# Five of seven Strassen products doubled in the first projection, and stick-breaking sums over later keys taken as two split products

## The chip, the cores and the metric

The program runs on one core of one Trainium2 chip. The metric is device time in microseconds (us) of that core; the changed kernel is timed against the kernel shown here. Engines are named as in the profile: PE is the matrix engine's matmul row and PEld its weight loads, DVE the vector engine, ACT the scalar (activation) engine, POOL the GpSimd engine, SP the engine that issues most DMAs; q behind a name means its instruction queue.

## What is computed

One decoder layer over 512 tokens of width 2048, in float32. Cut to what matters here:

```python
h = rmsnorm(x, attn_norm_g)
proj = h @ w_in                       # 2048 x 9216: u, v_sgu, q, k, v_att, g_a, g_b
y_a = chunked_spatial_gating(gelu(u), rmsnorm(gelu(v_sgu)))
y_b = stick_breaking_attention(rmsnorm(q), rmsnorm(k), v_att)   # 8 heads of 128
x = x + (sigmoid(g_a) * (y_a @ w_up_a) + sigmoid(g_b) * (y_b @ w_up_b)) @ w_o
x = x + swiglu(rmsnorm(x))            # w_ffn_in 2048 x 11264, w_ffn_out 5632 x 2048
x = x + sigmoid(rmsnorm(x) @ w_ple_gate) * (p @ w_ple)

# in stick_breaking_attention, for a block of 128 queries:
z = q @ k.T * scale
log_1m = where(key < query, log_sigmoid(-z), 0)
tail = cumsum(log_1m, reverse=True) - log_1m      # the sum over later keys
w = where(key < query, exp(log_sigmoid(z) + tail), 0)
y = w @ v
```

## The kernel before

All activations are held transposed, features on the partitions and the 512 tokens along the row. A float32 operand is kept as two float32r parts: `hi`, a rounded copy made by ACT, and `lo`, the rest, made by DVE as source minus `hi`. A product of two operands is then three matmuls: hi·hi, hi·lo and lo·hi (`mm3`, L271 to L273).

**Units.** The five big products are cut into units that give 256 output features each. A unit runs over 8 forms (256 input features each). A form of kind "S" is prepared for Strassen's scheme: 7 products of 128x128 weight blocks with 128x256 activation blocks instead of 8. Weights come by two SP DMAs and a POOL DMA that adds to what has landed (L316, L318, L338); `Weights.steps` makes two more sums on DVE (L350) and splits everything (`whi` on ACT, L334; `wlo` on DVE, L331). Weights of two forms are handled together, so a unit consists of 4 calls of `Pair.add`, each with 7 products for two forms.

**Two ways of a product.** Where `Pair.doubled` is false, `add` calls `mm3` on 256 columns three times for each product and form, into half a bank of PSUM; `HALVES` says which half of the banks "a", "q", "z" and "y", so that a unit holds four banks. Where it is true (only the feed-forward input, w_ffn_in), the activation's hi and lo parts lie side by side, and one matmul of 512 columns with the hi weights gives both hi·hi and hi·lo into the two halves of a bank of the product's own (L628); a second one of 256 columns with the lo weights adds to the first half.

**Combining.** During the last `add` of a unit, a generator (`mix`, or `mix_doubled`) is advanced after each product and adds the products up to the four output blocks: ACT copies (L653, L684) and DVE additions (L656, L687) that read PSUM. There are 6 banks "ps" and 2 banks "small"; a bank is written again by a later unit only after its readers are done.

**The first projection** (L1141 on) has 36 units: rounds 0 to 3 of q, k, v (two heads each) with 14 gate units between, then 4 s and 4 u units of the spatial gating and two more gates. The units of the first round's q, k and v run plain (8 products); the other 33 are Strassen units that are not doubled.

**Attention** runs beside those units. `tick()` is called eight times in a unit and starts what is due: `beside(generator)` advances a generator, which yields the number of ticks until its next step. `attention` handles a head's key blocks j = 3, 2, 1, 0 with (4 - j)·128 queries each. `stage_a` computes the scores (L1007, float32), their softplus on ACT and two terms on DVE (L1016, L1018) and masks on POOL (L1020). `stage_b` sums over later keys with float32 matmuls: a triangle for the block's own keys (L1030), and a matrix of ones times `later`, the running sum of later blocks (L1032); then it subtracts (L1034), keeps `later` up to date (POOL L1040, DVE L1042), takes the exponential and masks (L1045). `finish` multiplies with v (L1054).

**Storage and order.** `parts` and `wholes` are two arenas in SBUF; `take` chooses a place by first fit, aligned, from the end, or oldest given back. In a `tick` a form that is ready is fetched or built only if the arenas have room (`fits`). Instructions stand on each engine in an order fixed when the program is built: a scheduler sets it from priorities and dependences, `in_turn` chains the instructions on weights and in the mixes, and `tick` puts its own behind the unit's latest.

## Time and profile before

| what | value |
|---|---|
| runs | 2717.98, 2718.68, 2721.21 us, median 2718.68 |
| the profiled execution | 2719.95 us |
| its span, first to last instruction | 2718.3 us |
| mean granted clock of PE | 0.997 |
| PE busy | 2693.0 us, 99% of the span |
| DVE, ACT, POOL busy | 2075.1, 1353.5, 449.2 us |

The three runs differ by 3.2 us, and the profiled execution lies 1.3 us over their median. In the profile, busy time of PE comes from pipelined matmuls whose ends are modelled: a 256-column matmul shows 0.28 us but the next one begins 0.12 us later. What a matmul costs is therefore read from one start to the next. Columns in a timeline are start, duration, engine, line, operation and operands; in a table of lines, busy us, mean ns of one, and idle time before it with what ended it.

### The profile page before, as it was taken

The numbers are of one execution on the slowest core, as the hardware profiler recorded it, in microseconds if no ns is written. First come the engines' busy times: TensorE is split into PE (matmuls) and PEld (weight loads), VectorE is DVE, ScalarE is ACT, GpSimd is POOL, SyncE is SP. The second block draws the span as 40 slices with busy tenths as digits, with TensorE's granted clock in tenths as the row PEclk, the third lists the DMA queues.
The fourth block names the chain that finished last, engine by engine and source line by source line (L and its number), as shares of the span: only waits on it lengthen the run. The fifth ranks groups of instructions, "written<-read, shape, count | busy, mean of one in ns | idle before, by whom it ended". The sixth has DMA issues, their size and how long they took to land.

```text
span 2718.3 us, 45582 instructions
## 1 busy us (share of the span) xinstructions
PE 2693.0 (99%) x17243; PEld 2438.9 (90%) x17243; DVE 2075.1 (76%) x3377; ACT 1353.5 (50%) x2045; POOL 449.2 (17%) x527
## 2 busy tenths in 40 slices
PE   9999999999999999999999999999999999999999
PEld 7899999999999889988888888888888999989898
DVE  8566767667777667678889898989899567788876
ACT  7645556565554334365444444444445344453543
POOL 0222322232320000001111111111111111111110
PEclk9999999999999999999999999999999999999999
DMA  7567676767776447768888888887877669778784
GB/s 227 153 180 176 170 175 172 176 175 185 173 193 195 140 138 227 201 192 200 219 208 203 201 205 201 203 203 202 204 196 225 174 168 258 197 242 239 240 232 117
DMA packets 303132, 529.03 MB, mean 195 GB/s; under 512 B 25664, under 2 KB 162880, under 8 KB 302912
## 3 DMA queue, kind: packets, MB, share of 16 engines
q1 hardware_dynamic: 242160, 425.70, 49.0%
q0 software_dynamic: 60752, 100.43, 23.6%
q8 instruction: 135, 2.21, 0.3%
q14 instruction: 85, 0.70, 0.1%
HBM read 478.84 MB, written 47.19 MB: 194 GB/s over the span
## 4 chain that ended last, share of the span: by engine, by line
PE 95%; DMA 2%; DVE 1%; ACT 1%; issue 1%; POOL 0%; SPq 0%; ACTq 0%; DVEq 0%; POOLq 0%
PE ps L628 26%; PE ps L272 20%; PE ps L271 20%; PE ps L273 20%; PE small L628 4%; PE small L1054 1%; PE small L946 1%; PE small L1030 1%; PE small L1007 1%; DMA wholes<-x 0%; PE small L1032 0%; DMA ple<-out 0%; DVE wlo L331 0%; ACT whi L334 0%; PE small L1108 0%
## 5 line engine op out<-in xcount | busy, mean ns | idle before, releaser
L271 PE MATMUL ps<-parts,whi 128*128 128x256 f32 (+1 forms) x3995 | 1247.1, 314 | 13.3 <-ACT parts L266 7.4
L334 ACT ACTIVATE whi<-wholes 128x512 fp32r<-128x512 f32 (+4 forms) x950 | 856.1, 917 | 793.6 <-PE ps L272 305.3
L272 PE MATMUL ps<-parts,whi 128*128 128x256 f32 (+1 forms) x3960 | 1231.9, 311 | 1.3 <-DVE parts L267 1.3
L273 PE MATMUL ps<-parts,wlo 128*128 128x256 f32 (+1 forms) x3960 | 1230.4, 311 | 0.3 <-DVE wlo L331 0.3
L331 DVE TENSOR_TENSOR wlo<-wholes,whi 128x512 fp32r<-128x512 f32 (+4 forms) x950 | 964.9, 1050 | 156.5 <-ACT whi L334 155.0
L271 PEld LDWEIGHTS ps<-parts,whi 128*128 128x128 f32 x3995 | 764.2, 191 | 62.1 <-ACT parts L266 7.6
L272 PEld LDWEIGHTS ps<-parts,whi 128*128 128x128 f32 x3960 | 758.0, 191 | 44.7 <-DVE parts L267 2.2
L273 PEld LDWEIGHTS ps<-parts,wlo 128*128 128x128 f32 x3960 | 757.6, 191 | 38.9 <-DVE wlo L331 0.8
L628 PE MATMUL ps<-parts,whi 128*128 128x512 f32 x2064 | 683.2, 396 | 0.0
L628 PEld LDWEIGHTS ps<-parts,wlo 128*128 128x128 f32 x2064 | 387.9, 188 | 89.6
L628 PE MATMUL ps<-parts,wlo 128*128 128x256 f32 x2064 | 406.4, 278 | 0.0
L350 DVE TENSOR_TENSOR wholes<-wholes 128x256 f32<-128x256 f32 (+1 forms) x794 | 329.6, 415 | 27.5 <-issue 4.3
L628 PEld LDWEIGHTS ps<-parts,whi 128*128 128x128 f32 x2064 | 330.0, 189 | 2.1
L338 POOL DMA_DIRECT2D wholes<-w_ffn_in x172 | 149.7, 870 | 688.9 <-DVE wholes L350 229.7
L338 POOL DMA_DIRECT2D wholes<-w_in x132 | 118.8, 903 | 510.4 <-DMA wholes<-w_in 222.5
L687 DVE TENSOR_TENSOR out<-out,ps 128x256 f32<-128x256 f32 x258 | 107.6, 417 | 83.1 <-ACT out L684 83.0
L656 DVE TENSOR_TENSOR out<-out 128x256 f32<-128x256 f32 x59 | 25.0, 425 | 173.1 <-ACT out L653 172.8
L628 PE MATMUL small<-parts,whi 128*128 128x512 f32 x344 | 136.6, 397 | 0.0
L267 DVE TENSOR_TENSOR parts<-wholes,parts 128x1024 fp32r<-128x1024 f32 (+4 forms) x131 | 123.7, 953 | 14.0 <-ACT parts L266 13.5
L266 ACT ACTIVATE parts<-wholes 128x1024 fp32r<-128x1024 f32 (+4 forms) x131 | 105.7, 834 | 39.6 <-DVE wholes L497 15.6
L338 POOL DMA_DIRECT2D wholes<-w_ffn_out x56 | 57.0, 1031 | 401.0 <-DMA wholes<-w_ffn_out 187.5
L1299 ACT ACTIVATE out<-out 128x512 f32<-128x512 f32 x44 | 27.8, 633 | 161.2 <-DVE out L1298 161.2
(119 smaller groups left out, 1645.1 us busy)
## 6 DMA issues: line engine op xcount, KB each, us to landing
wholes<-w_ffn_in SPq DMA_DIRECT2D x172, 384.0 KB, 5.4
wholes<-w_in SPq DMA_DIRECT2D x132, 384.0 KB, 4.7
wholes<-w_ffn_in SPq DMA_DIRECT2D x172, 256.0 KB, 4.7
wholes<-w_ffn_in POOLq DMA_DIRECT2D x172, 256.0 KB, 5.2
wholes<-w_in SPq DMA_DIRECT2D x132, 256.0 KB, 3.8
wholes<-w_in POOLq DMA_DIRECT2D x132, 256.0 KB, 4.8
wholes<-x SPq DMA_DIRECT2D x32, 512.0 KB, 5.6
wholes<-w_ffn_out SPq DMA_DIRECT2D x31, 512.0 KB, 4.5
```

The source lines that it names most:

```text
L266: return (nc.scalar.activation(hi, src, AF.Copy), nc.vector.tensor_tensor(out=lo, in0=src, in1=hi.bitcast(F32), op=ALU.subtract))
L267: nc.vector.tensor_tensor(out=lo, in0=src, in1=hi.bitcast(F32), op=ALU.subtract))
L271: nc.tensor.matmul(ps[:, s], sh, mh[:, s], start=start, stop=False)
L272: nc.tensor.matmul(ps, sh, ml, start=False, stop=False)
L273: return nc.tensor.matmul(ps, sl, mh, start=False, stop=stop)
L331: in_turn(nc.vector.tensor_tensor(out=self.lo[:, blocks], in0=r, in1=h.bitcast(F32), op=ALU.subtract))
L334: in_turn(nc.scalar.activation(h, r, AF.Copy))
L338: nc.gpsimd.dma_start(out=raw[:, 3:5], in_=self.src[:, 1:3], accum_op=ALU.add)
L350: in_turn(nc.vector.tensor_tensor(out=o, in0=x, in1=y, op=ALU.add))
L628: m = nc.tensor.matmul(out, l, r, start=first and k == 0, stop=last and k == 1)
L687: in_turn(nc.vector.tensor_tensor(out=out, in0=x, in1=y, op=op))
L1299: nc.scalar.activation(g, g, AF.Silu)
```

## The change

In the first projection, the 33 Strassen units get `doubled=5`: the first five of the seven products (`PRODUCTS`) use one 512-column and one 256-column matmul each, as the feed-forward input does for all seven; the last two still use three 256-column matmuls and share the bank "y". A unit so holds six banks. `mix_doubled` combines five doubled products and that bank. `mix`, which the mixed units of later stages use, adds with three 256-column additions in place of one of 512 columns over two blocks, and needs no buffer of its own.

In attention, a block's masked terms are split into two float32r parts, `zh` (ACT, L1058) and `zl` (DVE, L1062). The sums over later keys are two float32r matmuls with a triangle of ones (L1068, L1069). The row of key 0, which no triangle of strictly later keys needs, carries later blocks' sums: POOL keeps the block's own first row (L1054) and clears it (L1055), and DVE puts into the next block's row 0 what row 0 of this block's result gives (L1071); the triangle for these blocks has ones in row 0 (`tris[1]`). `later` and the product with ones are gone. The steps go in threes of ticks through all eight blocks of a round's two heads, and attention begins 6 ticks after the k unit instead of 5 after the v unit. q is made in an `out` tile, and its normalised form goes to `y_b`.

The arenas change: `parts` is 1024 columns larger, `wholes` 512 smaller, alignment is to two places, and gates are loaded to the lowest place.

On PE, at the sums of a round's block j = 0 (`small` is the bank of the sums, `ps` a unit's bank); before:

```order
L272 MATMUL ps_1074<-parts,whi_80 128x256
L273 MATMUL ps_1074<-parts,wlo_81 128x256
L1030 MATMUL small_1305<-wholes,tri 128x512
L1032 MATMUL small_1305<-wholes,ones 128x384
L271 MATMUL ps_1103<-parts,whi_80 128x256
L272 MATMUL ps_1103<-parts,whi_80 128x256
L273 MATMUL ps_1103<-parts,wlo_81 128x256
```

and after, in such a place:

```order
L273 MATMUL ps_2941<-parts,wlo_77 128x256
L1068 MATMUL small_3121<-parts,tri_123 128x512
L629 MATMUL ps_3132<-parts,whi_80 128x512
L629 MATMUL ps_3132<-parts,wlo_81 128x256 x2
L629 MATMUL ps_3132<-parts,whi_80 128x512
L629 MATMUL ps_3137<-parts,whi_80 128x512
L629 MATMUL ps_3137<-parts,wlo_81 128x256 x2
L629 MATMUL ps_3137<-parts,whi_80 128x512
L1069 MATMUL small_3121<-parts,tri_123 128x512
L629 MATMUL ps_3142<-parts,whi_80 128x512
```

Six matmuls of a product for two forms became four, and the second product of the sums stands two products of the unit behind the first.

On DVE, the last `add` of a unit with a block of attention beside it (`out` is the unit's result, `p` its spare buffer); before:

```order
L656 TENSOR_TENSOR out_3030<-out_3030 128x256
L331 TENSOR_TENSOR wlo_81<-wholes,whi_80 128x1280
L331 TENSOR_TENSOR wlo_81<-wholes,whi_80 128x512
L656 TENSOR_TENSOR out_3030<-out_3030,p_283_3037 128x256
L656 TENSOR_TENSOR out_3030<-out_3030,p_283_3037 128x2x256
L1034 TENSOR_TENSOR wholes<-wholes,small_3067 128x512
L656 TENSOR_TENSOR out_3030<-out_3030,ps_2871 128x256
L656 TENSOR_TENSOR out_3030<-ps_2878,out_3030 128x512
```

and after, from the second addition of the mix:

```order
L688 TENSOR_TENSOR out_3066<-out_3066,ps_2909 128x256
L688 TENSOR_TENSOR out_3066<-out_3066 128x256
L688 TENSOR_TENSOR out_3066<-out_3066,ps_2914 128x256
L331 TENSOR_TENSOR wlo_79<-wholes,whi_78 128x1280
L331 TENSOR_TENSOR wlo_79<-wholes,whi_78 128x512
L688 TENSOR_TENSOR out_3066<-out_3066 128x256
L688 TENSOR_TENSOR p_347_3071<-p_347_3071,ps_2925 128x256
L1062 TENSOR_TENSOR parts<-wholes,parts 128x512
L688 TENSOR_TENSOR out_3066<-out_3066,ps_2936 128x256
L688 TENSOR_TENSOR out_3066<-out_3066,p_347_3071 128x2x256
L688 TENSOR_TENSOR out_3066<-out_3066,ps_2936 128x256
L688 TENSOR_TENSOR out_3066<-ps_2941,out_3066 128x512
```

The mix has ten DVE instructions instead of five, and the `lo` part of attention's terms (L1062) stands among them.

On SP, at the end of the first projection (`y` are attention's results, read back as operands of the next stage); before:

```order
L314 DMA wholes<-w_up_b 128x1024 x2
L1225 DMA gsp_8878<-out_8823 128x1024
L314 DMA wholes<-w_up_a 128x1024
L479 DMA wholes<-y_129 128x1024
L479 DMA wholes<-y_128 128x1024
L314 DMA wholes<-w_up_a 128x1024
```

and after:

```order
L314 DMA wholes<-w_up_b 128x1024 x2
L1253 DMA gsp_7991<-out_7939 128x1024
L314 DMA wholes<-w_up_a 128x1024
L479 DMA wholes<-y_132 128x1024
L314 DMA wholes<-w_up_a 128x1024
L314 DMA wholes<-w_up_b 128x1024
L479 DMA wholes<-y_133 128x1024
L479 DMA wholes<-y_134 128x1024
```

The last two reads of `y` stand two weight loads later.

The diff, cut:

```diff
-PARTS = 16 * PLACE
-WHOLES = 13824
+PARTS = 16 * PLACE + 1024
+WHOLES = 13312
...
-                    start = -(-start // PLACE) * PLACE
+                    start = -(-start // (2 * PLACE)) * 2 * PLACE
...
-            self.doubled = doubled and not self.n["P"]
+            self.doubled = 0 if self.n["P"] else doubled
...
-                    if self.doubled:
+                    if i < self.doubled:
                         ps = self.at(i)
                         both = ps, wh[:, w], t[:, x].rearrange("p s c -> p (s c)")
                         low = ps[:, :256], wl[:, w], t[:, x, 0]
...
-            copy(s, "q")
-            tt(b[:, 2], b[:, 1], s7)
-            tt(b[:, 1:4:2], b[:, 1:3], s5.unsqueeze(1).to_broadcast([P, 2, 256]))
+            copy(o[:, T:], "q")
+            tt(b[:, 2], b[:, 1], b[:, 2])
+            tt(b[:, 1], b[:, 1], b[:, 3])
+            tt(b[:, 3], b[:, 2], b[:, 3])
...
-            tt(c11, p2[0], c11, sub)
-            yield
-            tt(c12, p3[0], c12, sub)
-            tt(c11, c11, p2[1], add)
-            tt(c12, c12, p3[1], add)
+            if ps:
+                p2, p3 = ps
+                tt(c11, p2[0], c11, sub)
+                yield
+                tt(c12, p3[0], c12, sub)
+                tt(c11, c11, p2[1], add)
+                tt(c12, c12, p3[1], add)
+            else:
+                yield
+                tt(o[:, :T], self.at("y"), o[:, :T], sub)
...
+        def stage_m(h, j):
+            l, s, w = a_tile("l")[:, : (NT - j) * P], sums(j), weights(h, j)
             nc.vector.scalar_tensor_tensor(out=w, in0=s, scalar=0.0, in1=l,
                                            op0=ALU.min, op1=ALU.subtract)
             nc.vector.scalar_tensor_tensor(out=s, in0=s, scalar=0.0, in1=l,
                                            op0=ALU.max, op1=ALU.add)
             nc.gpsimd.affine_select(out=s[:, :P], in_=s[:, :P], pattern=[[1, P]],
...
+            if j < NT - 1:
+                if j:
+                    nc.gpsimd.tensor_copy(first(j), s[0:1])
+                nc.gpsimd.memset(s[0:1, :P], 0.0)
+
+        def stage_b(j):
+            nc.scalar.activation(zh[:, : (NT - j) * P], sums(j), AF.Copy)
+
+        def stage_c(j):
             n = (NT - j) * P
-            sp, w = state.pop((h, j))
-            later = state.get((h, "later"))
-            tp = small_bank()[:, :n]
-            nc.tensor.matmul(tp, tri, sp, start=True, stop=j == NT - 1)
-            if j < NT - 1:
-                nc.tensor.matmul(tp[:, P:], ones, later[:, j * P :], start=False,
-                                 stop=True)
+            in_turn(nc.vector.tensor_tensor(out=zl[:, :n], in0=sums(j), in1=att["zh"].f(0, n),
+                                            op=ALU.subtract))
+
+        def stage_d(h, j):
+            n, w = (NT - j) * P, weights(h, j)
+            tp, t = small_bank()[:, :n], tris[j < NT - 1]
+            nc.tensor.matmul(tp, t, zh[:, :n], start=True, stop=False)
+            nc.tensor.matmul(tp, t, zl[:, :n], start=False, stop=True)
+            if j:
+                nc.vector.tensor_tensor(out=sums(j - 1)[0:1, P:], in0=tp[0:1], in1=first(j),
+                                        op=ALU.add)
             nc.vector.tensor_tensor(out=w, in0=w, in1=tp, op=ALU.subtract)
-            if j == NT - 1:
-                later = a_tile("later", 3 * P)
-                state[h, "later"] = later
-            if j > 0:
-                c = j * P
-                nc.gpsimd.tensor_copy(later[:, c - P : c], sp[:, :P])
-                if j < NT - 1:
-                    nc.vector.tensor_tensor(out=later[:, c:], in0=later[:, c:], in1=sp[:, P:],
-                                            op=ALU.add)
             nc.scalar.activation(w, w, AF.Exp)
...
+        blocks = [(h, j) for h in range(2) for j in range(NT - 1, -1, -1)]
+        stage_a(*blocks[0])
+        yield 1
+        stage_m(*blocks[0])
+        yield 1
+        stage_a(*blocks[1])
+        for i, (h, j) in enumerate(blocks):
+            ahead = blocks[i + 1 : i + 3]
+            stage_b(j)
             yield 1
-            stage_b(h, 3)
+            if i == NT:
+                finish(0)
+            stage_c(j)
+            if ahead:
+                stage_m(*ahead[0])
             yield 1
-            stage_a(h, 1)
+            stage_d(h, j)
+            if ahead[1:]:
+                stage_a(*ahead[1])
             yield 1
...
-            yield pair(xs, last=i == len(srcs) - 1, home=lambda: block(*order[i]))
+            yield pair(xs, last=i == len(srcs) - 1, home=lambda: block(*order[i]),
+                       doubled=5)
...
+            beside(attention(i, kT, rk, a_tile("v", 1024)), 6)
...
-            s = load(gate_spill[b, j], PLACE if b == "a" and OUT[j] == "S" else 1024)
+            s = load(gate_spill[b, j], PLACE if b == "a" and OUT[j] == "S" else 1024,
+                     "low")
```

More of the change, by code (lines that the diff above doesn't have):

```diff
@@ L475, in cut, with load @@
         return x.rearrange("p (b c) -> p b c", c=256)
-    def load(src, n=1024):
-        b = take(n, "old")
+    def load(src, n=1024, how="old"):
+        b = take(n, how)
         nc.sync.dma_start(out=b.f(0, 1024), in_=src)
@@ L835, in hybrid_layer @@
     nc.vector.memset(ones, 1.0)
-    tri = consts.tile([P, P], F32, name="tri")
+    tris = [consts.tile([P, P], F32R, name=f"tri{i}") for i in range(2)]
+    tri = tmp.tile([P, P], F32, tag="diag", name="tri")
     nc.gpsimd.affine_select(out=tri, in_=ones, pattern=[[-1, P]], compare_op=ALU.is_gt,
                             fill=0.0, base=0, channel_multiplier=1)
+    nc.vector.tensor_copy(tris[0], tri)
+    nc.vector.memset(tri[0:1, :], 1.0)
+    nc.vector.tensor_copy(tris[1], tri)
     expo = consts.tile([P, 8], F32, name="expo")
@@ L931, in a_tiles @@
     def a_tiles():
-        for tag, n in (("l", T), ("later", 3 * P), ("w0", T), ("w1", 3 * P), ("w2", 2 * P), ("w3", P),
-                       ("k", 1024), ("v", 1024), ("zs", 1024)):
+        for tag, n in (("l", T), ("w0", T), ("w1", 3 * P), ("w2", 2 * P), ("w3", 2 * P),
+                       ("first", 5 * P), ("k", 1024), ("v", 1024), ("zs", 1024)):
             att[tag] = take(n)
+        for tag in ("zh", "zl"):
+            att[tag] = parts.take(T, "high")
     def a_tile(tag, n=T, start=0):
@@ L982, in q_prep @@
             yield 2
-            nc.scalar.activation(s, flip(q.f()), AF.Copy, scale=gcol[:, g_q : g_q + 1])
+            if not h:
+                y_b[i] = take(1024)
+            nc.scalar.activation(y_b[i].f(h * T, (h + 1) * T), flip(q.f()), AF.Copy,
+                                 scale=gcol[:, g_q : g_q + 1])
             give(q)
@@ L995, in v_prep, with attention, sums, weights @@
             times(v[:, h * T : (h + 1) * T], flip(o[:, h * T : (h + 1) * T]), norm1.cols)
-    def attention(rnd, qT, kT, rk, v):
+    def attention(rnd, kT, rk, v):
         state = {}
         yield 1
-        turn = [0]
+        qT = y_b[rnd].f()
+        zh, zl = (att[t].own() for t in ("zh", "zl"))
+        def sums(j):
+            return a_tile("zs", (NT - j) * P, j % 2 * T)
+        def weights(h, j):
+            return a_tile(f"w{j}", (NT - j) * P, (j == NT - 1) * h * P)
+        def first(j):
+            return (sums(j) if j == NT - 1 else a_tile("first", (NT - j) * P, (j == 1) * 2 * P))[0:1]
         def stage_a(h, j):
@@ L1203, in hybrid_layer @@
         if w == "q":
-            qT = o
-            beside(q_prep(qT))
+            beside(q_prep(o, i))
         elif w == "k":
@@ L1306, in hybrid_layer @@
     for m in range(KH):
-        o = pair(fs, last=m == KH - 1, plain=m == 0, doubled=True).out()
+        o = pair(fs, last=m == KH - 1, plain=m == 0, doubled=7).out()
         if m == 0:
```

56 lines of the change are left out of this document (16 added, 40 removed).

## The prediction

> **What bounds the kernel now.** I read the page's busy times first, then the chain that ended last, then the list of what PE waited for, and then the two stretches of the program that do Strassen units in the two ways.
>
> ```profile
> PE 2693.0 (99%) x17243; PEld 2438.9 (90%) x17243; DVE 2075.1 (76%) x3377; ACT 1353.5 (50%) x2045; POOL 449.2 (17%) x527
> ...
> PE 95%; DMA 2%; DVE 1%; ACT 1%; issue 1%; POOL 0%; SPq 0%; ACTq 0%; DVEq 0%; POOLq 0%
> ```
>
> The first row is busy time by engine, the second the shares of the chain. PE is the bound: whatever shortens its instruction stream shortens the program, as long as nothing makes it wait. What it waits for is little:
>
> ```profile
> PE small L946 <- ACT wholes L968: 2.2, 1, 2.2
> ...
> PE small L1054 <- POOL wholes L1045: 1.7, 4, 0.4
> ...
> PE small L1007 <- DVE wholes L1034: 0.2, 1, 0.2
> ```
>
> The columns are us in total, times, longest. In these three rows attention's own work holds PE for 4.1 us, of which the first round's query preparation is 2.2. No row has L1030 or L1032 waiting, the two matmuls that the change replaces.
>
> ```profile
> 125.00:835.00 710.00, 708.27 (x5636) 685.33 (x5635) 498.88 (x803) 395.72 (x725) 184.63 (x232) 1.00 0.71 178
> 1200.00:1500.00 300.00, 299.14 (x1679) 259.27 (x1678) 259.07 (x462) 152.47 (x216) 54.16 (x61) 0.99 0.85 216
> 80.00:160.00 80.00, 77.17 (x567) 72.35 (x566) 51.80 (x91) 52.41 (x120) 23.85 (x33) 0.98 0.65 166
> ```
>
> These are stretches with busy us of PE, PEld, DVE, ACT and POOL, then the granted clock. The first holds nearly all of the 33 Strassen units of the first projection: PE is busy for 708.27 of 710 us, DVE for 70%. The second lies in the feed-forward input, where all seven products are doubled: DVE is at 86%, and PE still loses less than 1 us in 300. The third contains the 2.2 us wait and has a clock of 0.98: 2% of 80 us is another 1.6 us that this stretch lost.
>
> **Doubling five products.** The price of a unit is read from unit to unit, where nothing else uses PE. In the first projection the first copy of the mix comes once in a unit:
>
> ```profile
> 801.76 0.60 ACT L653 ACTIVATE out<-ps 128x512 f32<-128x512 f32 x1 [1.00 <-PE ps L273]
> ...
> 821.92 0.60 ACT L653 ACTIVATE out<-ps 128x512 f32<-128x512 f32 x1 [0.96 <-PE ps L273]
> ```
>
> In the feed-forward input, the same place of two units in the chain:
>
> ```profile
> 1350.64 4.19 PE ps L628 x24
> ...
> 1370.16 4.19 PE ps L628 x24
> ```
>
> 20.16 us against 19.52 us: seven doubled products save 0.64 us in a unit. From one start to the next, the single matmuls say the same:
>
> ```profile
> 299.72 0.28 PE L271 MATMUL ps<-parts,whi 128*128 128x256 f32 x1
> 299.84 0.28 PE L272 MATMUL ps<-parts,whi 128*128 128x256 f32 x1
> ...
> 1389.76 0.40 PE L628 MATMUL ps<-parts,wlo 128*128 128x256 f32 x2
> 1390.00 0.63 PE L628 MATMUL ps<-parts,whi 128*128 128x512 f32 x2
> 1390.46 0.40 PE L628 MATMUL ps<-parts,wlo 128*128 128x256 f32 x2
> ```
>
> A matmul of 256 columns takes 0.12, so an old product of one form takes 0.36; two doubled ones take 1390.46 - 1389.76 = 0.70, or 0.35 each, which leaves 0.23 for 512 columns. The gain is the third weight load, not columns, of which there are 768 either way. Five of seven products give 0.64 x 5/7 = 0.46 us in a unit, and 33 units give **-15.1 us**. The ends are 0 (were it columns alone) and 15.1; I take 15.1, because the same operation with the same shapes was measured beside it.
>
> The Trainium skill speaks against this: "TensorE: Matmul & The Clock Gate", section Back-to-back issue gap, gives an isolated warm matmul N/2.4 + 2.5 ns. An estimate from that page: three of 256 columns take 327.5 ns, 512 and 256 together 325.0, so 33 x 40 products of one form would save 3.3 us. By that rule 256 columns take 109 ns; the trace has 120, and does not agree.
>
> **Attention's sums.** Before, a block's two float32 matmuls appear as four records. What they put into the stream is the distance between the first of them and the second of the unit's matmuls behind, less that unit matmul's 0.12:
>
> ```profile
> 174.55 1.02 PE L1030 MATMUL small<-wholes,tri 128*128 128x512 f32 x2
> 175.41 0.81 PE L1032 MATMUL small<-wholes,ones 128*128 128x384 f32 x2
> 175.76 0.58 PE L271 MATMUL ps<-parts,whi 128*128 128x256 f32 x1
> 176.18 0.28 PE L272 MATMUL ps<-parts,whi 128*128 128x256 f32 x1
> ...
> 161.90 0.60 PE L1030 MATMUL small<-wholes,tri 128*128 128x256 f32 x2
> 162.34 0.38 PE L1032 MATMUL small<-wholes,ones 128*128 128x128 f32 x2
> 162.48 0.36 PE L271 MATMUL ps<-parts,whi 128*128 128x256 f32 x1
> 162.68 0.28 PE L272 MATMUL ps<-parts,whi 128*128 128x256 f32 x1
> ...
> 116.49 0.39 PE L1030 MATMUL small<-wholes,tri 128*128 128x128 f32 x2
> 116.63 0.36 PE L271 MATMUL ps<-parts,whi 128*128 128x256 f32 x1
> 116.83 0.28 PE L272 MATMUL ps<-parts,whi 128*128 128x256 f32 x1
> ```
>
> That is 1.51 us for j = 0 (896 columns), 0.66 for j = 2 (384 columns) and 0.22 for j = 3 (128); j = 1 has 640 columns, and at the 1.7 ns a column of the other two takes 1.08. A head pays 3.47 us. After, the pairs of float32r matmuls have 512, 384, 256 and 128 columns: 0.46 and 0.24 for the first and third by the rows above, 0.35 for 384 between them. For 128 float32r columns there is no row; the pair lies between 0.12 (half of the 256-column one) and 0.44 (the float32 one twice), and I take 0.24, since the rows at 0.12 with one weight load each look bound by it. A head then pays 1.29, and eight heads gain 8 x 2.18 = **-17.5 us**, with ends 16 and 18.5.
>
> **What is added beside PE.** Prices from the groups by form, and medians for a line in all its sizes:
>
> ```profile
> L687 DVE TENSOR_TENSOR out<-out,ps 128x256 f32<-128x256 f32 x258 | 107.6, 417 | 83.1 <-ACT out L684 83.0
> L684 ACT ACTIVATE out<-ps 128x256 f32<-128x256 f32 x129 | 49.5, 384 | 29.4 <-PE ps L628 26.5
> L653 ACT ACTIVATE out<-ps 128x512 f32<-128x512 f32 x59 | 35.1, 595 | 41.0 <-PE ps L273 40.5
> L656 DVE TENSOR_TENSOR out<-out,p 128x512 f32<-128x512 f32 x59 | 40.8, 692 | 1.8
> L1034 DVE TENSOR_TENSOR wholes<-wholes,small x32: 280/480/689, 118.9 to 618.6; 128x128 f32<-128x128 f32 x8, 128x256 f32<-128x256 f32 x8, 128x384 f32<-128x384 f32 x8, 128x512 f32<-128x512 f32 x8
> L1012 ACT ACTIVATE wholes<-small,rr x32: 353/527/683, 110.4 to 609.0; 128x128 f32<-128x128 f32 x8, 128x256 f32<-128x256 f32 x8, 128x384 f32<-128x384 f32 x8, 128x512 f32<-128x512 f32 x8
> L1020 POOL TENSOR_SCALAR_AFFINE_SELECT wholes<-wholes 128x128 f32<-128x128 f32 x32 | 14.5, 453 | 66.0 <-DVE wholes L1018 56.5 <-PE ps L272 9.5
> L1040 POOL COPY wholes<-wholes 128x128 f32<-128x128 f32 x24 | 15.8, 660 | 1.3
> ```
>
> The mix of a unit had three DVE additions of 256 columns and two of 512 (3 x 0.417 + 2 x 0.692 = 2.64 us); it gets eight and two (4.72), so 33 units cost DVE 69 us. Attention adds 32 subtractions for `zl` (0.480 each, as L1034: 15.4) and 24 additions of one row (on average 256 columns: 10.0), and loses 16 additions to `later` (128 and 256 columns, 5.6). DVE goes from 498.88 to some 587 us in a stretch that shrinks to 677: 87%, what the feed-forward input carries with PE full. ACT gets four copies of 256 for two of 512 (+0.35 a unit) and 32 copies for `zh` (0.527 each): 424 us, 63%. POOL loses 24 copies (15.8) and gets 16 of one row and 24 clearings; with 0.66 for each that is 195 us, 29%. All of this is hidden by PE's stream; if the cover went, DVE's 69 us would be the first to show. The mixed units of later stages (36) pay 0.14 each on DVE, beside a PE that has more than enough work. A unit's six banks: the one of product i is wanted again a unit later, and its readers come within the last `add`; the feed-forward input holds its six the same way without a wait.
>
> **The new waits.** The sums now hang on a chain DVE, POOL, ACT (`zh`), DVE (`zl`), PE, and the next block's chain on the row that DVE adds behind it. `zl` stands in DVE's fixed order among weight splits and the longer mix, and PE stands still at L1069 until it is there; the unit's products queue behind. Bounds: nothing, if PE's stream covers it, and 32 x (0.527 + 0.480) = 32.2 us, if both splits are exposed in every block. The nearest rows are L1030, with a chain of DVE and POOL and no wait, and L1054 and L1007 with 1.9 us in all. The chain is longer by two links and DVE fuller, so I take an eighth of the upper end, **+4 us**.
>
> At the end of the stage, the order shows the last two reads of `y` two weight loads later. Before, they had room:
>
> ```profile
> 832.66 0.33 SPq L479 DMA_DIRECT2D wholes<-y  x1
> ...
> 839.15 1.23 DVE L267 TENSOR_TENSOR parts<-wholes,parts 128x1024 fp32r<-128x1024 f32 x1
> ...
> 853.66 0.39 PE L271 MATMUL ps<-parts,whi 128*128 128x512 f32 x1
> ```
>
> The last operand was split at 840.4 and first used at 853.66, so 13 us of cover stand against two loads of some 5 us (a unit of 20.16 us has four). I cost it at nothing; beyond the cover, it would be about 2 us of wait and 1.6 of clock, as in the third stretch above.
>
> **Sum.** 2719.95 (the profiled execution; its span is 2718.3) - 15.1 - 17.5 + 4 = 2691.4. That execution lies 1.3 us over the median of 2718.68, so against the runs I say **2690 us**.
>
> **Rivals.**
> - The doubled form brings little here, because the two products that stay undoubled break its rhythm, or because columns set the pace after all: 0 to 3 us instead of 15.1, so about 2703. Against it stand 20.16 and 19.52. Chance 0.12. The skill's rule above would give this result, from its 3.3 us.
> - Attention's chain is exposed by half, as DVE at 87% is late in the units whose mix coincides: 16 us in place of 4, so 2702. For it: the order has `zl` (L1062) right among the mix. Chance 0.12.
> - Slower: every block stands out in full, `zh`, `zl` and POOL's selection (0.453) ahead of them, 32 x 1.46 = 46.7 us: 2686 + 46.7 = 2733. It decides from 32.6 us on, 1.02 us in each block. Against it: PE's sums stand at least a product's time behind, and steps are a tick (2.5 us) apart. Chance 0.03.
> - Better than forecast: no new waits, and the 1.9 us of the old ones vanish: 2684. Chance 0.05.
>
> **Chances.** The forecast, 2684 to 2697, gets 0.68. The range 2684 to 2704 takes in the first two rivals' centres and leaves out the slower case and their far ends, some 0.15. A measurement of this kernel can tell about 0.2% (5.4 us) from no change: faster than that 0.94, within it 0.03 (the chain exposed nearly in full), slower 0.03.
>
> **What would show it.** In the profile after: units without attention 19.70 us apart; 40 matmuls of 512 columns in each unit, none of L1032; pairs L1068 and L1069 with 0.46 us between first and last for 512 columns; DVE near 87% from 125 to 800 us; waits of PE on L1062 or L1058 of some 4 us in all. I would be wrong if PE waited at L1069 for about 1 us in each block, if units stayed at 20.16, or if the stages behind 850 us changed by more than 3 us.

## The result and the profile after

The changed kernel took 2705.2 us, the median of runs between 2703.6 and 2709.7 us; runs of the kernel before beside it had a median of 2718.3 us. The ratio is 0.9943, with a 95% interval of 0.9926 to 0.9961, which is 2703.2 us against the 2718.68 us of the prediction. The kernel became faster by about 15 us, where 28.7 were forecast: the forecast time is 13 us too low, and the result lies inside the range, 0.8 us below its upper end.

From the page after, busy time by engine and the shares of the chain that ended last; then the first projection in the window that was read before, and the feed-forward input:

```profile
PE 2668.1 (99%) x15875; PEld 2354.6 (87%) x15875; DVE 2147.0 (79%) x3621; ACT 1367.3 (51%) x2143; POOL 459.0 (17%) x543
...
PE 88%; DVE 5%; DMA 2%; ACT 2%; issue 1%; POOL 1%; SPq 0%; DVEq 0%; ACTq 0%; POOLq 0%
```
```profile
125.00:815.00 690.00, 682.72 (x4351) 607.93 (x4350) 563.94 (x1003) 411.11 (x824) 198.35 (x253) 1.00 0.74 182
1180.00:1480.00 300.00, 300.00 (x1689) 260.37 (x1689) 264.33 (x473) 156.56 (x221) 53.29 (x61) 1.00 0.85 217
```

PE is still the bound, but DVE's share of the chain went from 1% to 5%, and in the first projection PE now stands idle for 7.3 of 690 us, where it lost 1.7 of 710. DVE is at 82% there (87% was forecast), less than in the feed-forward input, where it is at 88% and PE loses nothing. DVE's load by itself does not explain the waits, then.

The list of what PE waited for in the first projection (us in total, times, longest) names the places:

```profile
PE small L1069 <- DVE parts L1062: 3.6, 4, 0.9
PE small L959 <- ACT wholes L981: 2.5, 1, 2.5
PE small L1084 <- POOL wholes L1075: 2.2, 4, 0.6
PE small L1034 <- ACT wholes L981: 0.7, 3, 0.2
PE small L1141 <- ACT wholes L981: 0.5, 1, 0.5
PE ps L629 <- DVE p L688: 0.3, 1, 0.3
PE ps L272 <- DVE parts L267: 0.2, 1, 0.2
```

L959, L1084 and L1034 are the old L946, L1054 and L1007; 2.2, 1.7 and 0.2 us became 2.5, 2.2 and 0.7. The largest new row is L1069, the second product of the sums: four waits of 0.9 us, one in each round, at block j = 0 of the second head. The timeline of one of them (start, duration, engine, line; in brackets the idle time before it and what ended it):

```profile
315.27 0.64 ACT L1058 ACTIVATE parts<-wholes 128x512 fp32r<-128x512 f32 x1 [2.01 <-DVE wholes L1071]
...
317.78 0.75 DVE L688 TENSOR_TENSOR out<-out,ps 128x256 f32<-128x256 f32 x2 [1.47 <-ACT out L685]
...
319.24 2.18 DVE L331 TENSOR_TENSOR wlo<-wholes,whi 128x1280 fp32r<-128x1280 f32 x2
...
321.47 0.39 PE L629 MATMUL ps<-parts,whi 128*128 128x512 f32 x1
...
322.01 0.68 DVE L1062 TENSOR_TENSOR parts<-wholes,parts 128x512 fp32r<-128x512 f32 x1
...
322.74 0.50 PE L1069 MATMUL small<-parts,tri 128*128 128x512 f32 x1 [0.88 <-DVE parts L1062]
```

`zh` was done at 315.91, and soon after DVE stood idle for 1.47 us (until 317.78). But `zl` has its place behind six additions of the mix and two weight splits of 2.18 us together, and so it ran at 322.01, six us after it could. From the start of the matmul ahead to that of L1069 are 1.27 us, 1.04 more than its 0.23.

To compare kernels, each trace is cut at three starts on PE: its first matmul, the first of the Strassen units, and the first of w_up (behind that, all kernels here have the same 10,895 PE instructions). "Plain" is the stretch ahead of the second cut, "part" that of the Strassen units up to the third, "behind" the rest up to the start of the last matmul. The names are those of the experiments below.

```
kernel                                plain    part   behind   timed against before
before                                80.66  759.91  1867.31
changed                               82.06  738.40  1870.88   0.9943 (0.9926 to 0.9961)
e1_double_only                        80.86  751.86  1864.09   0.9964 (0.9953 to 0.9976)
e2_att_only                           82.30  748.80  1871.17   0.9963 (0.9951 to 0.9975)
e3_zl_early                           83.10  742.72  1868.85   0.9956 (0.9943 to 0.9969)
e4_fin_late                           82.85  736.80  1873.22   0.9932 (0.9919 to 0.9944)
e5_storage                            83.51  749.70  1873.93   0.9991 (0.9983 to 1.0000)
e6_cover0                             82.42  740.00  1875.48   0.9949 (0.9936 to 0.9962)
e7_cover0_fin                         82.56  742.77  1873.20   0.9939 (0.9927 to 0.9952)
e8_double7                            81.34  747.40  1876.21   0.9977 (0.9968 to 0.9986)
e9_low                                80.16  751.20  1874.67   0.9987 (0.9978 to 0.9995)
e10_zl0_fin                           83.09  735.86  1871.81   0.9931 (0.9919 to 0.9943)
e11_phase5                            81.65  738.35  1874.37   0.9940 (0.9928 to 0.9952)
e12_high                              80.40  735.69  1874.88   0.9951 (0.9937 to 0.9964)
```

Between the first two profiles the part gained 21.5 us, and 1.4 and 3.6 us were given back ahead of it and behind it: 16.5 us in all, against the 2719.95 - 2703.6 = 16.35 of the two profiled executions. A cut stretch of one execution carries its chance stalls, so differences under 2 us say little by themselves.

The granted clock is one of these chances. Every trace has stretches of 3.4 us with a granted clock of 0.50 (below, stretches at the lower clock), and one of them costs about 1.7 us (an estimate, 3.4 x 0.50). In the part there is none in e3, e5 and e9, there are two in e7 and three in e8, and there is one in each of the other kernels. Behind it there are three in the kernel before and in the changed one, one in e1 and e9, two in e2 and e3, and three to five in the others (one of 6.8 us counts as two).

### The profile page after: what moved, and what is told of

Its sections match the earlier page's. It is cut to its first block, busy times and chain, and to the rows that moved or that the text cites. A ratio compares the mean times of both kernels' runs of the same rounds, so it can differ in the third digit from the quotient of the medians.

```text
span 2701.9 us, 43167 instructions
## 1 busy us (share of the span) xinstructions
PE 2668.1 (99%) x15875; PEld 2354.6 (87%) x15875; DVE 2147.0 (79%) x3621; ACT 1367.3 (51%) x2143; POOL 459.0 (17%) x543
## 4 chain that ended last, share of the span: by engine, by line
PE 88%; DVE 5%; DMA 2%; ACT 2%; issue 1%; POOL 1%; SPq 0%; DVEq 0%; ACTq 0%; POOLq 0%
PE ps L629 39%; PE ps L272 14%; PE ps L273 14%; PE ps L271 14%; PE small L629 4%; DVE wlo L331 2%; DVE out L688 1%; PE small L1084 1%; PE small L959 1%; ACT whi L334 1%; DMA wholes<-w_in 0%; DMA wholes<-w_first 0%; DVE wholes L350 0%; PE small L1034 0%; DVE parts L267 0%
## 5 line engine op out<-in xcount | busy, mean ns | idle before, releaser
L629 PE MATMUL ps<-parts,whi 128*128 128x512 f32 x3384 | 1134.8, 398 | 0.3 <-DVE p L688 0.3
L271 PE MATMUL ps<-parts,whi 128*128 128x256 f32 (+1 forms) x2675 | 855.1, 323 | 15.7 <-ACT parts L266 9.7
L272 PE MATMUL ps<-parts,whi 128*128 128x256 f32 (+1 forms) x2640 | 857.0, 325 | 1.0 <-DVE parts L267 0.8
L273 PE MATMUL ps<-parts,wlo 128*128 128x256 f32 (+1 forms) x2640 | 855.9, 325 | 0.9 <-DVE wlo L331 0.9
L629 PE MATMUL ps<-parts,wlo 128*128 128x256 f32 x3384 | 671.1, 279 | 0.0
L271 PEld LDWEIGHTS ps<-parts,whi 128*128 128x128 f32 x2675 | 508.8, 190 | 60.7 <-ACT parts L266 10.8
L629 PEld LDWEIGHTS ps<-parts,whi 128*128 128x128 f32 x3384 | 545.3, 189 | 5.0 <-issue 1.0
L272 PEld LDWEIGHTS ps<-parts,whi 128*128 128x128 f32 x2640 | 502.7, 191 | 47.2 <-DVE parts L267 2.8
L688 DVE TENSOR_TENSOR out<-out,ps 128x256 f32<-128x256 f32 x388 | 160.3, 415 | 131.7 <-ACT out L685 131.5
L655 DVE TENSOR_TENSOR out<-out 128x256 f32<-128x256 f32 x144 | 60.9, 423 | 114.7 <-ACT out L652 112.2
L266 ACT ACTIVATE parts<-wholes 128x1024 fp32r<-128x1024 f32 (+4 forms) x131 | 105.8, 834 | 42.0 <-DVE wholes L497 20.0
```

The costliest lines, as they stand in the source:

```text
L266: return (nc.scalar.activation(hi, src, AF.Copy), nc.vector.tensor_tensor(out=lo, in0=src, in1=hi.bitcast(F32), op=ALU.subtract))
L271: nc.tensor.matmul(ps[:, s], sh, mh[:, s], start=start, stop=False)
L272: nc.tensor.matmul(ps, sh, ml, start=False, stop=False)
L273: return nc.tensor.matmul(ps, sl, mh, start=False, stop=stop)
L629: m = nc.tensor.matmul(out, l, r, start=first and k == 0, stop=last and k == 1)
L655: in_turn(nc.vector.tensor_tensor(out=out, in0=x, in1=y, op=op))
```

## The experiments

**The two halves of the change alone.** First the doubled products with their mix, put into the kernel before; then the changed kernel without them:

```diff
-            yield pair(xs, last=i == len(srcs) - 1, home=lambda: block(*order[i]))
+            yield pair(xs, last=i == len(srcs) - 1, home=lambda: block(*order[i]),
+                       doubled=5)
```

> The kernel before with the five doubled products (and their mix) alone: old attention, old arenas. The Strassen part is the stretch from the first Strassen matmul of the first projection to the first matmul of w_up: 759.9 us before, 738.4 after. Theory A (the two parts add up; a unit gains the 0.37 us that the units without attention show, 20.16 - 19.79): 33 x 0.37 = 12.2 us, so 747.7 us there, no new wait of PE above 0.5 us, and about 2706 us in all. Rival B (the fuller DVE costs already here): PE waits on L1030 or its kind appear, and the part stays above 751 us. Rival C (a unit gains the forecast 0.46 us and attention's waits eat it): 744.8 us. Behind the part, Theory A says nothing changes (within 1 us), if the later stages' 3.6 us in the changed kernel come from its new storage.

```diff
-            yield pair(xs, last=i == len(srcs) - 1, home=lambda: block(*order[i]),
-                       doubled=5)
+            yield pair(xs, last=i == len(srcs) - 1, home=lambda: block(*order[i]))
```

> The changed kernel with the first projection's products not doubled: new attention and new arenas alone. Theory A (attention's missing 8 us are PE waits that come from the fixed place of zl on DVE and of the last product with v, not from the longer mix): the Strassen part falls from 759.9 by about 9 us to 751 us, and PE still waits on L1062 for 3 to 4 us in all. Rival B (the longer mix of the doubled units makes the waits): no such waits, 742.5 us. Behind the part: +3.6 us as in the changed kernel, if storage sets it; about 0, if it was chance of one execution.

The part became 8.1 and 11.1 us shorter, with the whole change 21.5; the two together are 2.3 us short of it. For the doubling, Rival B has the size (751.9) and half the mechanism: the missing 4 us stand in new waits, but not attention's:

```profile
PE small L1114 <- ACT wholes L974: 2.2, 1, 2.2
PE small L952 <- ACT wholes L974: 2.0, 1, 2.0
PE ps L629 <- DVE p L688: 1.6, 2, 1.0
PE small L1060 <- POOL wholes L1051: 1.6, 1, 1.6
```

L952 and L1060 are the old L946 and L1054, with 3.6 us where they had 3.9. L1114, a product of the spatial gating, and the mix's L688 are new: 3.8 us. In the changed kernel the same two places cost 0.8, so it is no fixed price of the longer mix. Which step is late also changes with the execution or with the loads: the run e9_low below, with the same order of instructions on PE, DVE, ACT and POOL up to w_up, has 0.7 us at L1114 and 4.8 at L1060. For attention, Theory A expected 751 us and Rival B 742.5; 748.8 is nearer the first. Without the longer mix PE still waits:

```profile
PE small L959 <- ACT wholes L981: 2.6, 1, 2.6
PE small L1069 <- DVE parts L1062: 2.0, 4, 1.5
PE small L1034 <- ACT wholes L981: 2.0, 3, 0.7
PE small L1034 <- ACT wholes L998: 0.7, 1, 0.7
```

The waits belong to attention's own chain, as Theory A says, but in part at other steps: 2.0 at L1069 in place of 3.6, and 2.7 at L1034 in place of 0.7.

**zl earlier.** All of `zl` in the tick of `zh`:

```diff
             stage_b(j)
+            stage_c(j)
             yield 1
             if i == NT:
                 finish(0)
-            stage_c(j)
```

> The changed kernel with zl (L1062) started in the same tick as zh, one tick earlier, so that it stands on DVE ahead of the mix and the weight split. Theory A: PE's waits on L1062 (4 x 0.9 us by the list of waits) vanish, the Strassen part falls by 3.6 to 4.2 us to about 734.5 us, and nothing else changes. Rival B: DVE, full at 82%, only moves the lateness to the mix or to the weights (PE waits on L331 or on banks in their place): the part stays within 1 us of 738.4.

```profile
PE small L1084 <- POOL wholes L1075: 6.6, 7, 1.6
...
PE ps L629 <- DVE out L688: 1.5, 3, 0.5
PE ps L629 <- DVE p L688: 1.5, 4, 0.6
```

L1069 is gone from the list, and yet the part is 4.3 us longer than in the changed kernel, though it holds no stretch at the lower clock and the changed kernel's holds one. Rival B had the direction, not the size: the waits moved to the product with v (6.6 us) and to the banks that the mix gives back (3.0 us).

**The product with v later.**

```diff
-        yield 1
+        yield 2
         finish(1)
```

> The changed kernel with the second head's product with v one tick (2.5 us) later. Theory A: PE's waits at that product (4 x 0.6 us on POOL L1075 by the list of waits) vanish, the Strassen part falls by about 2.2 to 2.9 us to 735.8 us. Rival B: PE waits elsewhere for the same (the bank of the sums, or q's normalisation): no change, 738.4 us.

The waits at L1084 vanished, those at L1069 stayed (4.0 us in all), and the part fell by 1.6 us, less than the 2.2 expected; L1141 waits for 1.1 us where it had 0.5, and L1069 for 0.4 more. Theory A holds, though 1.6 us of one execution is little. The ratio 0.9932 is not told apart from 0.9943 by the runs alone.

**The sums later.** A tick more ahead of the sums of j = 0, alone and with the later product with v:

```diff
-            yield 1
+            yield 1 if j else 2
             stage_d(h, j)
```

> The changed kernel with one tick more between zl and the sums, for block j = 0 of each head alone. Theory A (PE waits at L1069 only since zl has too little time there; the work itself fits): the waits on L1062 (3.6 to 4.0 us) vanish, the product with v waits as before, the Strassen part falls from 738.4 by 4.2 us to 734.2 us. Rival B (as with the earlier zl, the time is given back at another wait, on POOL's mask L1075 or on the banks of the mix): the part stays at 737 us or above.

> The two later steps together: the sums of j = 0 a tick later and the second head's product with v a tick later. Theory A (both waits go, they are independent): Strassen part 738.4 - 4.2 - 1.6 (what the second alone gained) = 732.6 us, about 2698.5 us in all when the rest is as in the changed kernel. Rival B: they are one wait seen twice, 734 to 735 us.

In both the part stayed above 737 us, as Rival B of the first says: 740.0 and 742.8 us. Neither theory of the second run names that time (its second stretch at the lower clock is some 1.7 us of it). The wait of j = 0 went, and the second head, now a tick later against its units, waits at j = 1 instead, as the list of the first run shows:

```profile
PE small L1068 <- ACT parts L1058: 2.6, 4, 0.7
...
PE ps L629 <- DVE out L688: 1.7, 4, 0.5
PE small L1069 <- DVE parts L1062: 1.7, 4, 0.4
```

**zl earlier for j = 0 alone, and another phase.** The first moves only the `zl` of j = 0, in both heads, and has the later product with v; the second leaves the order within attention as in the run with the later product and starts all of it a tick sooner:

```diff
             stage_b(j)
+            if not j:
+                stage_c(j)
             yield 1
             if i == NT:
                 finish(0)
-            stage_c(j)
+            if j:
+                stage_c(j)
```

> The changed kernel with zl in zh's tick for block j = 0 of each head alone, and the second head's product with v a tick later. Theory A (only the zl of j = 0 stands badly; the other blocks' zl, moved too in the earlier experiment, made that one slower): no wait on L1062 above 0.5 us, Strassen part 736.8 - 4.2 = 732.6 us. Rival B (zl ahead of the mix delays the mix, and PE waits for its banks on L688): 735 to 738 us.

```diff
-            beside(attention(i, kT, rk, a_tile("v", 1024)), 6)
+            beside(attention(i, kT, rk, a_tile("v", 1024)), 5)
```

> The second head's product with v a tick later, and all of attention started one tick earlier (5 after the k unit instead of 6), so that the zl of the second head's j = 0 stands on DVE ahead of the mix, and every other block stands otherwise against its unit too. Theory A (the waits are a matter of where steps fall against the mix): the 4 waits on L1062 of about 1 us go; those of other blocks change; together -2 to -4 us, 733 to 735 us. Rival B (another block comes into the mix in its place): 736.8 us or more, with new waits at L1069 or L1068 of other sizes.

In the first, the DVE timeline at the place shown above reads:

```profile
314.20 0.69 DVE L1062 TENSOR_TENSOR parts<-wholes,parts 128x512 fp32r<-128x512 f32 x1 [0.30 <-ACT parts L1058]
...
316.04 0.75 DVE L688 TENSOR_TENSOR out<-out,ps 128x256 f32<-128x256 f32 x2 [0.26 <-ACT out L685]
```

`zl` is through before the mix begins, and no wait on L1062 is left in the list. The part is 735.9 us, in Rival B's range and not the 732.6 of Theory A: 0.9 us less than 736.8 for 4.0 us of waits removed, too little to be told from chance. But the mix is not what took it (L688 waits for 0.9 us in all, where it had 0.3); the list now has L1144, the spatial gating's product, with 2.0 us, and L1084 again with 1.7. These two rows are not a fixed price either: the last kernel below (e12_high) has the same order on PE, DVE, ACT and POOL up to w_up, and there they are 0.2 and 3.5 us, in a part of 735.7. So which step took the removed waits is not settled. The other phase removed L1069's wait as well (0.2 us left) and put 4.2 us at L1084, in eight waits: 738.4 us. That is Rival B's time, but at another step than the L1068 or L1069 that it named. Of the six runs on attention's waits (the last two taken against the run with the later product), only the later product with v turned most of the waiting that it removed into a shorter part; the other five turned less than a quarter of it into time, or the part became longer.

**All seven products doubled.**

```diff
-                       doubled=5)
+                       doubled=7)
```

> The changed kernel with all seven products of the first projection's units doubled; the seventh takes one of attention's two banks. Theory A (a doubled pair costs 0.351 us here against 0.360 for three, whatever stands beside it): units without attention fall from 19.79 to 20.16 - 56 x 0.009 = 19.66 us. Rival B (the two products that stayed undoubled cost the difference to the feed-forward input): 19.52 us as there. For the time, the bank decides: if attention does well with one bank, the Strassen part falls by 33 x 0.13 = 4.3 us to 734 us; if its scores and sums now wait for each other, each of 32 blocks may lose up to 1 us and the part rises to 750 us or more. I expect the second.

Once in a unit the mix's first copy comes; in the changed kernel and then in this one, units without attention:

```profile
801.69 0.39 ACT L685 ACTIVATE out<-ps 128x256 f32<-128x256 f32 x1 [0.23 <-PE ps L629]
...
821.47 0.39 ACT L685 ACTIVATE out<-ps 128x256 f32<-128x256 f32 x1 [0.44 <-PE ps L629]
```
```profile
790.77 0.39 ACT L685 ACTIVATE out<-ps 128x256 f32<-128x256 f32 x1
...
829.81 0.39 ACT L685 ACTIVATE out<-ps 128x256 f32<-128x256 f32 x1 [0.28 <-PE ps L629]
```

19.78 us, and 39.04 us for two units or 19.52 for one: with seven doubled, a unit takes what it takes in the feed-forward input, to 0.01 us, and Rival B is right. A unit with five is 0.08 us slower than its share (20.16 - 0.46 = 19.70). The starts of these units show where: a doubled pair takes 0.349 us on average in a unit of seven, and 0.351 in a unit of five; three single matmuls take 0.36, in a unit of five as in the kernel before. Why, no row shows. For the time the waits decided, as expected: the part rose to 747.4 us, with some 3.4 us of the rise from two more stretches at the lower clock.

```profile
PE small L1141 <- ACT wholes L981: 7.2, 4, 2.6
PE small L959 <- ACT wholes L981: 6.0, 4, 4.0
PE small L1034 <- DVE wholes L1073: 3.2, 4, 1.2
```

All three write one of the two small banks, of which the seventh product now holds one through its unit; that they wait for this reason is argued from the program, not shown by a row.

**The time outside the part.** The doubled products alone, with the changed kernel's storage; then with the old arenas, and only the gates' place changed (the last three lines of this diff); then the kernel of e10_zl0_fin with the gates at the highest place:

```diff
-PARTS = 16 * PLACE
-WHOLES = 13824
+PARTS = 16 * PLACE + 1024
+WHOLES = 13312
...
-                    start = -(-start // PLACE) * PLACE
+                    start = -(-start // (2 * PLACE)) * 2 * PLACE
...
-            s = load(gate_spill[b, j], PLACE if b == "a" and OUT[j] == "S" else 1024)
+            s = load(gate_spill[b, j], PLACE if b == "a" and OUT[j] == "S" else 1024,
+                     "low")
```

> The doubled products alone once more, with the old attention, but now with the changed kernel's storage: arenas of the new sizes, alignment to two places, gates loaded to the lowest place. Theory A (the time lost outside the Strassen part comes from storage, which moves loads and builds): against the run with the doubled products and the old storage, the plain units before the part get 1.2 to 2.4 us longer (80.9 to 82.1-83.3 us), the output stage behind ffn_out and the last 1000 matmuls together 2 to 5 us longer, as in all four kernels with the new storage, and the Strassen part itself stays within 1.5 us of 751.9 us. Rival B (it comes from attention's code: the triangles' preparation at the start, y read back later): nothing outside the part changes by more than 0.5 us.

> The doubled products alone, old attention, arenas of the old sizes and alignment; only the gates are loaded to the lowest place. Theory A (the smaller arena of the weights' landings moves the loads at the start; the gates' place moves those of the later stages): the plain units take 80.9 us as with the old storage, and the later stages lose most of what the run with the whole new storage lost (some 4 of its 7 us behind the part). Rival B (the sizes do all of it): the later stages stay within 1 us of the run with the old storage.

```diff
-                     "low")
+                     "high")
```

> The run with the earlier zl of j = 0 and the later product with v (Strassen part 735.9 us there), with the gates loaded to the highest free place instead of the lowest; all else equal. The stretch from the first matmul of w_up to the last of the program takes 1764 to 1767 us with the old storage and 1769 to 1776 us with the new. Theory A (the gates' place decides it): about 1766 us, and 2697 us in all. Rival B (the smaller arena alone moves the late loads as much): 1770 us or more, 2702 us in all. The part before stays within 1 us of 736 us by both.

Storage alone makes e1_double_only slower by the ratios' difference, 0.9991 - 0.9964 = 0.0027 or 7.3 us, with intervals that do not touch. By the cuts it is 2.7 us in the plain units and 9.8 behind, with 2.2 us less in the part. That is Theory A in its direction, with all three past its bounds (1.2 to 2.4 us, 2 to 5 in two places, and 1.5). The cuts show 3 us more than the ratios; the profiled execution of e1_double_only was the fastest of its five, 3.1 us under their median. Two more stretches at the lower clock are some 3.4 of the 9.8 us, and the one that e1_double_only has in its part some 1.7 of the 2.2. What PE waited for behind the part, with the old storage and with the new (9.2 and 14.3 us in all), in the longest rows:

```profile
PE ps L271 <- ACT parts L483: 2.0, 1, 2.0
PE ps L271 <- ACT parts L266: 1.8, 1, 1.8
```
```profile
PE ps L271 <- ACT parts L266: 6.1, 3, 3.4
PE ps L271 <- ACT whi L334: 1.9, 2, 1.1
```

L266 is the ACT copy that makes an operand's `hi` part. The gates' place alone leaves the plain units at 80.2 us and the part at 751.2, and costs 10.6 us behind by the cuts and 6.3 by the ratios, with one stretch at the lower clock behind as in e1_double_only (Theory A; more than the "some 4" it named). So the gates' place by itself moves the later stages, and the sizes move the start. On PE, the order of e9_low leaves that of e1_double_only only at 1189 us, that of e5_storage at 22 us. Of the eleven kernels with the new sizes ten have plain units of 81.3 to 83.5 us and one, the last run, 80.4, against 80.2 to 80.9 in the three with the old. But no simple cure follows: in the last run, whose expectation gives the stretch behind 100 us too low throughout by a slip in adding (1864 to 1867 is meant for the old storage, 1869 to 1876 for the new), the highest place gave 1874.9 us, on Rival B's side, with 735.7 in the part and 0.9951 in all. The order of the late loads on SP differs in all three; which of them is late, and why, was not settled.

## Why the prediction was half right

- **Doubling, -15.1.** The mechanism held: 512 columns and 256 in place of three times 256. The term was mis-sized, since units without attention took 19.78 us and not 19.70: 33 x 0.38 is 12.5 us. Unit by unit, 17 of the 33 in e1_double_only gain 0.34 to 0.40 us over the kernel before; the others have waits or other work in them. "Five of seven products give 0.64 x 5/7" was the failed step; a unit with two kinds of products is not the mean of two pure units. The rival "the two products that stay undoubled break its rhythm" was right in kind and a fifth of its size. The formula of the Trainium skill ("TensorE: Matmul & The Clock Gate", Back-to-back issue gap), by which the estimate was 3.3 us, is not borne out: 12.5 us came.
- **Attention's sums, -17.5.** The prices came as assumed. From the first product of a pair to the matmul behind the pair:

```profile
259.37 0.31 PE L1068 MATMUL small<-parts,tri 128*128 128x128 f32 x1
...
259.62 0.44 PE L629 MATMUL ps<-parts,whi 128*128 128x512 f32 x1
...
268.27 0.28 PE L1068 MATMUL small<-parts,tri 128*128 128x256 f32 x1
...
268.51 0.59 PE L1034 MATMUL small<-wholes 128*128 128x512 f32 x1
...
295.76 0.22 PE L1068 MATMUL small<-parts,tri 128*128 128x128 f32 x1
...
295.93 0.54 PE L1034 MATMUL small<-wholes 128*128 128x384 f32 x1
...
312.66 0.34 PE L1068 MATMUL small<-parts,tri 128*128 128x384 f32 x1
...
313.01 0.40 PE L629 MATMUL ps<-parts,whi 128*128 128x512 f32 x1
```

  The pairs of 256 and 384 columns take 0.24 and 0.35 us. That of 128 took 0.17 in second heads (295.76 to 295.93) and 0.25 in first ones (259.37 to 259.62). For j = 0 the two products stand apart and take 0.46 together where nothing waits (0.235 and 0.226 us for the block at 149.03 us). So a head pays 1.26 on average, and eight heads gain 17.7 us. (The 8 x 2.18 of the prediction is 17.4, not 17.5.)
- **New waits, +4.** The part gained 21.5, so what is left for waits is 12.5 + 17.7 - 21.5 = 8.7 us, more than twice the term; it is a remainder, not a measurement. The place and its idle time were named rightly (L1069 behind `zl` in DVE's fixed order, 3.6 us of "some 4"). But the list in all adds 10.0 - 4.1 = 5.9 us, since the old waits grew as well, and a wait costs more from start to start than the list shows (1.04 for 0.88); the rest of the 8.7 is not assigned. "An eighth of the upper end" was no reading of the program: in the order printed ahead of the prediction, one `zl` stands behind additions of the mix and the two splits that take 2 us.
- **Outside the part, 0.** The prediction costed the changed arenas at nothing and looked only at the two later reads of `y`, which did no harm at that place. 1.4 us ahead and 3.6 behind were lost, past the 3 us behind that it had set as its own refutation. The clock is not the reason, since both traces have three stretches at the lower clock there, and the storage run shows that storage alone can cost as much.
- **Sum.** Against the profiled execution 2691.4 was forecast and 2703.6 came: 2.6 from the doubling, 4.7 from waits, 5.0 from outside, less 0.2 from attention's sums, is 12.1 of the 12.2 us; it has to come out nearly so, as the waits are a remainder. No rival stood alone: the first two happened in part, and the 5.0 us outside were in no rival. Three terms erred the same way, and that the time still fell inside the range, by 0.8 us, is luck.

The best kernels run, with the later product with v (0.9932) and with the earlier `zl` of j = 0 too (0.9931), have medians below the changed kernel's ratio, but within its interval.

## What to carry to other kernels

Where instructions stand in a fixed order on each engine, a step that is cheap and early can still be late: follow it through the order to what stands ahead of it, in each of its positions against the periodic work, before pricing a wait. A named wait of 1 us is a place, not a gain; taking it away shortened the part by little or not at all in five of six runs here, since other steps then waited. And a change of buffer sizes or placement moves loads in stages that the change doesn't touch, here at a price of 5 to 7 us, about as much as the 5.9 us of new waits in the list.

## What the runs showed of the hardware

A stall of 1.8 us may or may not cost the clock. The same wait in the timelines of the kernel before and of the changed one, and for each the granted clock (the third figure from the end) in a window of 3.5 us behind it:

```profile
2070.10 0.47 PE L271 MATMUL ps<-parts,whi 128*128 128x512 f32 x1 [1.81 <-DVE out L687]
```
```profile
2070.20:2073.70 3.50, 3.50 (x16) 2.89 (x17) 3.47 (x7) 0.97 (x2) 0.00 (x0) 1.00 0.73 235
```
```profile
2049.04 0.47 PE L271 MATMUL ps<-parts,whi 128*128 128x512 f32 x1 [1.81 <-DVE out L688]
```
```profile
2049.50:2053.00 3.50, 3.50 (x11) 2.70 (x10) 3.50 (x7) 1.25 (x2) 0.00 (x0) 0.53 0.63 200
```

At 0.53 the second loses another 1.6 us (an estimate, 3.5 x 0.47). In thirteen of the fourteen traces L271 waits 1.81 us at this place; behind ten of these waits a stretch at 0.50 begins within 1.3 us, behind three (the kernel before, e1_double_only and e9_low) none does. What decides it was not settled.

An addition on DVE over one partition is no cheaper here than one over 128: the row of 1x384 (L1071) took 0.54 us, and the block of 128x384 behind it (L1073) 0.53.

```profile
314.64 0.54 DVE L1071 TENSOR_TENSOR wholes<-small,wholes 1x384 f32<-1x384 f32 x1
...
315.44 0.53 DVE L1073 TENSOR_TENSOR wholes<-wholes,small 128x384 f32<-128x384 f32 x1
```
